# A decoder layer on one core: at the boundaries, two late squares go into the norm's sum on VectorE before TensorE sums over partitions

## The chip, the cores and the metric

The kernel runs on one core of a Trainium2 chip. A core has TensorE (PE, matrix products; PEld are its weight loads), VectorE (DVE), ScalarE (ACT), GpSimd (POOL) and SyncE (SP, which here only issues transfers). Each engine works through a queue of its own in order; they wait for each other by semaphores. The metric is the device time of one execution in microseconds.

## The reference

One decoder layer on x of 512 tokens by 1024 channels, float32. Each of three sub-layers is wrapped in two RMS norms:

```python
def rms_norm(x, g):
    y = x * lax.rsqrt(jnp.mean(x * x, axis=-1, keepdims=True) + NORM_EPS)
    return y * g

x = x + 0.5 * rms_norm(swiglu(rms_norm(x, g1), w1_in, w1_out), g1_post)
h = rms_norm(x, g2)
q, k, v, u = split(h @ w_mix_in)
mixed = concat(dilated_attention(q, k, v), s5_mixer(u)) @ w_mix_out
x = x + rms_norm(mixed, g2_post)
x = x + 0.5 * rms_norm(swiglu(rms_norm(x, g3), w2_in, w2_out), g3_post)
```

A norm needs, for every token, the sum of 1024 squares. That sum is what the change touches, at the two places where one sub-layer ends and the next begins.

## The kernel before

Activations lie transposed: channels on the 128 partitions, in 8 tiles of 128 channels (`KD` = 8), tokens along the free dimension. Every matrix product of full precision is done as three products of split operands (a high and a low half, `mm3` at L133): hence `whi`, `wlo`, `xh`, `xl` in the profile. All matmuls are issued in the written order (`mm`, L127). For other engines a planner lays out the order of each queue; `fix` (L120, `keep_in_program_order`) pins an instruction behind the one that was written before it for the same engine, and unpinned instructions go where the planner finds them ready.

`boundary` (L258) joins two sub-layers: from the first to the mix, and from the mix to the last. It works on two halves of 256 tokens (`HT`), h = 0 and 1:

- `product(h, m)` makes the last part of output tile m of the old sub-layer on TensorE (bank `yt`).
- `gather(h, m, n, b)` adds n tiles of it to `y` on VectorE (L287).
- `squares(h, m, n, eng)` squares them on ScalarE (L293) and adds the squares to `acc[h]` on the engine given (L296). Tiles 0 to 5 come in pairs: a pair's squares fill 512 columns, the even tile's in the first 256, the odd one's in the second. Tiles 6 and 7 come one by one.
- `fold` (L167) adds the second 256 columns of `acc` to the first, on GpSimd.
- `rstd` (L171) returns two steps. `sums` lets TensorE sum over the partitions (each 128x128 block of squares times a column of ones, into bank `st`), then VectorE scales (`nv`, L190) and GpSimd takes the power -1/2 (L192). `spread` lets TensorE spread the result over the partitions (bank `rp`).
- `prep(h, k)` makes tile k of the new sub-layer's input on VectorE and ScalarE: a multiply by `rp` (L302), an add to x (L304), the high half `xh` on ScalarE (L151), the low half `xl` on VectorE (L152), and its square for the next norm (ScalarE L161, added on GpSimd L163).
- `begin(h, k)` feeds that tile into the first four products of the new sub-layer (bank `first`): 12 matmuls.

In the second half the squares of tiles 0 to 5 go to `acc[1]`, which is folded after m = 5. The squares of tiles 6 and 7, 256 columns each, are not added to it: they go into the list `late`. `sums(late)` is called after `begin(0, 2)`. It lets TensorE sum three tiles into the same place: the folded `acc[1]`, and the two late ones, two blocks each, six matmuls. `spread` follows after `begin(0, 4)`, and then come `prep(1, k)` and `begin(1, k)` for k = 0 to 7.

Of the kernel before, what the change touches and what calls it, by code (L numbers as in the profile page):

```python
# [12 lines left out]
ALU = mybir.AluOpType  # L13
# [4 lines left out]
P = 128  # L18
# [10 lines left out]
HT = S // 2  # L29
# [11 lines left out]
class Layer:  # L41
# [78 lines left out]
    def fix(self, i):  # L120
        return self.tc.keep_in_program_order(i)
# [48 lines left out]
    def rstd(self, acc, y4, r, h0=0, h1=4, folded=False):  # L170

        nc = self.nc
        n = h1 - h0
        y = y4[:, h0:h1]

        def sums(more=(), fix=lambda i: i, fixp=None):

            st = self.bank("st")
            if folded and not more:
                self.fold(acc, nc.gpsimd, fixp or fix)
            t = [acc[:, 0 if folded else h0 * P:], *more]
            for i, ti in enumerate(t):
                for b in range(n):
                    self.mm(st[:, 2 * b:2 * b + 2], lhsT=ti[:, b * P:(b + 1) * P], rhs=self.ones,
                            start=i == 0 and b == 0, stop=i == len(t) - 1 and b == n - 1)
            v = self.sp.tile([P, 4], F32, name="nv", tag="nv")[:, :n]
            fix(nc.vector.tensor_scalar(out=v, in0=st[:, 0:2 * n:2], scalar1=1.0 / D, scalar2=EPS,  # L190
                                        op0=ALU.mult, op1=ALU.add))
            (fixp or fix)(nc.gpsimd.tensor_tensor(out=y, in0=v, in1=self.mhalf[:, :n], op=ALU.pow))  # L192

        def spread(fix=lambda i: i):
            rp = self.bank("rp")
            for b in range(n):
                self.mm(rp[:, b * P:(b + 1) * P], lhsT=y[:, b:b + 1].to_broadcast([P, P]),
                        rhs=self.ident, start=True, stop=True)
            if r is not None:
                fix(nc.scalar.copy(out=r[:, h0 * P:h1 * P], in_=rp[:, :n * P]))  # L200
            return rp[:, :n * P]

        return sums, spread

    def rtiles(self):
# [52 lines left out]
    def boundary(self, y, tail, ipost, half, inext, chunks):  # L258


        nc = self.nc
        w = [self.load(c, (KD, P), pool=i % 2 == 1) for i, c in enumerate(chunks)]
        tw = lambda i, m, k: self.tw[m // 2][i].rearrange("p (m k j) -> p m k j", k=NT, j=P)[:, m % 2, k]
        hs = [slice(0, HT), slice(HT, S)]
        xh, xl = self.ktiles("xh", F32R), self.ktiles("xl", F32R)
        acc2 = self.acct()
        n4, nr = self.rtiles()
        o = [self.bank("first") for _ in w]
        p4 = self.sp.tile([P, 4], F32, name="p4", tag="p4")
        bank, acc = [None], [self.acct(), self.acct()]  # L270
        post = [self.rstd(acc[h], p4, None, 2 * h, 2 * h + 2, True) for h in range(2)]
        rr = [None, None]
        pre = [self.rstd(acc2, n4, nr, 0, 2), self.rstd(acc2, n4, nr, 2, 4)]

        def product(h, m):
            if m % 2 == 0 or m == 7:
                bank[0] = self.bank("yt").rearrange("p (m t) -> p m t", m=2)
            b = bank[0][:, m % 2 if m < 6 else 0]
            for k in range(NT):
                th, tl = tail(k)  # L280
                self.mm3(b, tw(0, m, k), tw(1, m, k), th[:, hs[h]], tl[:, hs[h]], k == 0, k == NT - 1)
            return bank[0]

        def gather(h, m, n, b, fix=lambda i: i):

            ym = y.pair(slice(m, m + n))[:, :, hs[h]]
            fix(nc.vector.tensor_tensor(out=ym, in0=b[:, :n], in1=ym, op=ALU.add))  # L287

        def squares(h, m, n, eng, fix=lambda i: i):

            m2 = slice(m % 2, m % 2 + n)
            t = (acc[h] if m == 0 else self.tmp("sq")).rearrange("p (m t) -> p m t", m=2)[:, m2]
            fix(nc.scalar.activation(out=t, in_=y.pair(slice(m, m + n))[:, :, hs[h]], func=AF.Square))  # L293
            if m and eng:
                ac = acc[h].rearrange("p (m t) -> p m t", m=2)[:, m2]
                (fix if eng is V else fx)(eng.tensor_tensor(out=ac, in0=ac, in1=t, op=ALU.add))  # L296
            return t.rearrange("p m t -> p (m t)")

        def prep(h, k, fix=lambda i: i):
            t = y(k)[:, hs[h]]  # L300
            xk = self.x(k)[:, hs[h]]
            fix(nc.vector.scalar_tensor_tensor(out=t, in0=t, scalar=self.g(ipost, k, half), in1=rr[h],  # L302
                                               op0=ALU.mult, op1=ALU.mult))
            fix(nc.vector.tensor_tensor(out=xk, in0=t, in1=xk, op=ALU.add))  # L304
            self.split(xh(k)[:, hs[h]], xl(k)[:, hs[h]], xk, self.g(inext, k), fix)
            self.sq_acc(acc2[:, hs[h]], xk, k == 0, nc.gpsimd)

        def begin(h, k):
            for i in range(len(w)):
                self.mm3(o[i][:, hs[h]], w[i][0][:, k], w[i][1][:, k], xh(k)[:, hs[h]], xl(k)[:, hs[h]],  # L310
                         k == 0, k == KD - 1)

        V, G, fx = nc.vector, nc.gpsimd, self.fix
        b2 = [self.bank("yt")[:, :HT] for _ in range(2)]
        for ks in (range(NT - 1), (NT - 1,)):
            for m in range(2):
                for k in ks:
                    th, tl = tail(k)
                    self.mm3(b2[m], tw(0, m, k), tw(1, m, k), th[:, hs[0]], tl[:, hs[0]], k == 0, k == NT - 1)
        for m in range(2):  # L320
            gather(0, m, 1, b2[m].unsqueeze(1))
        squares(0, 0, 2, V)
        for m in range(2, KD):
            b = product(0, m)
            if m % 2 or m > 5:
                m, n = (m - 1, 2) if m < 6 else (m, 1)
                gather(0, m, n, b)
                squares(0, m, n, G if m == 2 else V)
        late = []
        for m in range(KD):  # L330
            b = product(1, m)
            if m % 2 or m > 5:
                m1, n = (m - 1, 2) if m < 6 else (m, 1)
                gather(1, m1, n, b)
                t = squares(1, m1, n, G if n == 2 else None)
                if n == 1:
                    late.append(t)
                if m == 5:
                    self.fold(acc[1], G, fx)
            if m == 2:  # L340
                post[0][0](fixp=fx)
            if m == 3:
                rr[0] = post[0][1]()
                for k in range(2):
                    prep(0, k)
        for k in range(KD):
            if k > 1:
                prep(0, k, fx if k > 5 else lambda i: i)
            begin(0, k)
            if k == 2:  # L350
                post[1][0](late, fix=fx)
            if k == 4:
                rr[1] = post[1][1]()
        for k in range(KD):
            prep(1, k)
            begin(1, k)
            if k == 3:
                pre[0][0](fixp=fx)
            if k == 6:
                pre[0][1]()  # L360
        self.xh, self.xl = xh, xl
        return o, n4, nr, pre[1]
# [876 lines left out]
```

## Time and profile before

| what | us |
|---|---|
| median of 3 runs (lowest, highest) | 960.45 (960.17, 960.68) |
| the profiled execution, its time | 959.66 |
| its span, from the first to the last instruction | 957.9 |
| TensorE busy | 940.9 |
| VectorE busy | 526.3 |
| ScalarE busy | 367.6 |
| GpSimd busy | 224.2 |

Times inside the trace count from the start of the span. The two boundaries lie at about 354 to 403 us and 556 to 604 us. In a row of the timeline stand the start, the duration, the engine, the line of the kernel, the operation, output and inputs, shapes and the count; in brackets is the time that the engine was idle before, and what it waited for. Matmuls overlap, so a row can start before the one ahead of it has ended; the spacing of the starts is what a matmul costs. A row of stretches gives the stretch, its length, the busy time of TensorE, its weight loads, VectorE, ScalarE and GpSimd with their counts, the granted TensorE clock (1.00 is full), the share of the DMA engines and GB/s.

### The profile page before, as it was taken

Reading aid. Unit: us, or ns where it says so; the run is one execution under the profiler, and the core shown is the slowest. Engines: PE = TensorE matmul, PEld = TensorE weight load, DVE = VectorE, ACT = ScalarE, POOL = GpSimd, SP = SyncE. Lnnn points to the kernel's source line nnn. Section 1 sums busy time; section 2 is a strip of 40 time slices with the busy share of each in tenths; the row PEclk is TensorE's granted clock in tenths of the full one; section 3 lists DMA queues with packets and bytes.
Section 4 is the critical chain, followed back from the end, with each engine's and each line's share of the span. In section 5 each row is a group of like instructions: output and inputs, shape, how many; then the busy total and the mean of one; then the engine's idle time right before and its main releaser. Section 6 shows DMA issues by size and latency. Waiting matters only on the chain.

```text
span 957.9 us, 12872 instructions
## 1 busy us (share of the span) xinstructions
PE 940.9 (98%) x5082; PEld 787.8 (82%) x5082; DVE 526.3 (55%) x934; ACT 367.6 (38%) x610; POOL 224.2 (23%) x134
## 2 busy tenths in 40 slices
PE   9999999999999999999999999999999999999995
PEld 7888888788888889988766899888888888888884
DVE  6998214463246446759896659644135524453427
ACT  7354334352233233435646645443233212232312
POOL 0234212322223233500000035421122212223300
PEclk9999999999999999999999999999999999999998
DMA  8233334353334241382313430323232232324202
GB/s 266 88 110 98 101 112 142 119 177 102 109 110 132 68 160 39 104 224 83 123 67 97 150 109 1 121 81 107 88 110 89 90 104 93 109 89 132 88 1 89
DMA packets 38173, 102.48 MB, mean 107 GB/s; under 512 B 7616, under 2 KB 10944, under 8 KB 37568
## 3 DMA queue, kind: packets, MB, share of 16 engines
q1 hardware_dynamic: 36528, 98.02, 31.6%
q10 hardware_dynamic: 1584, 3.63, 1.1%
q8 instruction: 40, 0.66, 0.3%
q14 instruction: 21, 0.17, 0.1%
HBM read 94.03 MB, written 7.60 MB: 106 GB/s over the span
## 4 chain that ended last, share of the span: by engine, by line
PE 88%; DVE 6%; ACT 2%; issue 1%; DMA 1%; POOL 0%; SPq 0%; POOLq 0%; DVEq 0%; ACTq 0%
PE gu L129 45%; PE yo L129 20%; PE yt L129 6%; PE first L129 5%; PE prj L129 3%; PE prv L129 2%; DVE wlo L104 1%; PE st L129 1%; PE ys L129 1%; PE gl L129 1%; DMA wraw<-w1i 1%; PE mo L129 1%; DVE Hs L1109 1%; DVE sx L1109 1%; PE pt L832 1%
## 5 line engine op out<-in xcount | busy, mean ns | idle before, releaser
L104 POOL TENSOR_TENSOR wlo<-wraw,whi 128x1024 fp32r<-128x1024 f32 (+2 forms) x62 | 157.3, 2537 | 496.9 <-ACT whi L102 496.8
L102 ACT CAST whi<-wraw 128x1024 fp32r<-128x1024 f32 (+5 forms) x157 | 154.6, 990 | 303.9 <-PE gu L129 118.7
L129 PE MATMUL gu<-xh,whi 128*128 128x512 f32 x656 | 257.7, 393 | 0.0
L129 PE MATMUL gu<-xh,wlo 128*128 128x512 f32 x656 | 255.7, 390 | 0.5 <-DVE wlo L104 0.5
L129 PE MATMUL gu<-xl,whi 128*128 128x512 f32 x656 | 255.3, 389 | 0.0
L104 DVE TENSOR_TENSOR wlo<-wraw,whi 128x1024 fp32r<-128x1024 f32 (+5 forms) x95 | 116.0, 1226 | 121.8 <-ACT whi L102 121.5
L129 PEld LDWEIGHTS gu<-xh,wlo 128*128 128x128 f32 x656 | 123.1, 188 | 27.0 <-DVE wlo L104 1.0
L129 PEld LDWEIGHTS gu<-xh,whi 128*128 128x128 f32 x656 | 123.2, 188 | 25.3 <-issue 0.4
L129 PEld LDWEIGHTS gu<-xl,whi 128*128 128x128 f32 x656 | 123.2, 188 | 24.9
L402 DVE TENSOR_TENSOR ut<-gu,rs 128x512 f32<-128x512 f32 x41 | 28.2, 688 | 102.8 <-PE gu L129 102.8
L149 DVE TENSOR_TENSOR al<-ut,ah 128x512 fp32r<-128x512 f32 x44 | 68.5, 1559 | 25.4 <-ACT ah L148 25.4
L400 DVE TENSOR_TENSOR gt<-gu,rs 128x512 f32<-128x512 f32 x41 | 28.2, 688 | 51.8 <-PE gu L129 51.8
L129 PE MATMUL yo<-whi,ah 128*128 128x512 f32 x144 | 56.0, 389 | 0.0
L129 PE MATMUL yo<-wlo,ah 128*128 128x512 f32 x144 | 56.0, 389 | 0.0
L129 PE MATMUL yo<-ah,whi 128*128 128x512 f32 x144 | 56.0, 389 | 0.0
L129 PE MATMUL yo<-ah,wlo 128*128 128x512 f32 x144 | 56.0, 389 | 0.0
L129 PE MATMUL yo<-whi,al 128*128 128x512 f32 x144 | 56.0, 389 | 0.0
L129 PE MATMUL yo<-al,whi 128*128 128x512 f32 x144 | 56.0, 389 | 0.0
L148 ACT CAST ah<-ut 128x512 fp32r<-128x512 f32 x44 | 27.3, 622 | 59.7 <-DVE ut L403 59.7
L129 PE MATMUL first<-xh,whi 128*128 128x256 f32 (+1 forms) x144 | 43.3, 301 | 0.4 <-ACT xh L151 0.4
L129 PE MATMUL first<-xl,whi 128*128 128x256 f32 (+1 forms) x144 | 42.6, 296 | 0.6 <-DVE xl L152 0.6
L129 PE MATMUL first<-xh,wlo 128*128 128x256 f32 (+1 forms) x144 | 42.4, 295 | 0.0
(194 smaller groups left out, 1401.9 us busy)
## 6 DMA issues: line engine op xcount, KB each, us to landing
wraw<-w2i SPq DMA_DIRECT2D x44, 512.0 KB, 3.4
wraw<-w1i SPq DMA_DIRECT2D x42, 512.0 KB, 3.5
wraw<-w2o SPq DMA_DIRECT2D x18, 512.0 KB, 3.4
wraw<-w1o SPq DMA_DIRECT2D x16, 448.0 KB, 3.4
wraw<-wmi SPq DMA_DIRECT2D x12, 512.0 KB, 3.6
x<-xT SPq DMA_DIRECT2D x8, 256.0 KB, 4.2
w1d<-w1s SPq DMA_DIRECT2D x8, 256.0 KB, 2.7
w2d<-zb SPq DMA_DIRECT2D x2, 1024.0 KB, 4.8
```

Source lines behind the costliest of these rows:

```text
L102: fix(self.nc.scalar.copy(out=hi, in_=raw))
L104: fix(eng.tensor_tensor(out=lo, in0=raw, in1=hi.bitcast(F32), op=ALU.subtract))
L129: i = self.nc.tensor.matmul(*a, **k)
L148: fix(nc.scalar.copy(out=hi, in_=src))
L149: fix(nc.vector.tensor_tensor(out=lo, in0=src, in1=hi.bitcast(F32), op=ALU.subtract))
L400: nc.vector.tensor_tensor(out=gt, in0=o[f][0], in1=r, op=ALU.mult)
L402: nc.vector.tensor_tensor(out=ut, in0=o[f][1], in1=r, op=ALU.mult)
L832: self.fix(nc.tensor.transpose(b[i][:, o:o + P], sc[:, c:c + P], self.ident))
L1109: tt = lambda o, x, y, op: self.fix(V.tensor_tensor(out=o, in0=x, in1=y, op=op))
```

## The change

The list `late` is gone. In the second half, the squares of tiles 6 and 7 are each added to the folded first 256 columns of `acc[1]` by VectorE, pinned behind what was written before them for VectorE (the gather of the same tile). `sums` always runs over one tile: two matmuls in place of six in the second half. Its first argument now only says whether it folds `acc` itself (the first half, `add=True`) or not (the second, `False`). The first half and the new sub-layer's own norms compute as before.

```diff
-        def sums(more=(), fix=lambda i: i, fixp=None):
+        def sums(add=True, fix=lambda i: i, fixp=None):
 
             st = self.bank("st")
-            if folded and not more:
+            if folded and add:
                 self.fold(acc, nc.gpsimd, fixp or fix)
-            t = [acc[:, 0 if folded else h0 * P:], *more]
-            for i, ti in enumerate(t):
-                for b in range(n):
-                    self.mm(st[:, 2 * b:2 * b + 2], lhsT=ti[:, b * P:(b + 1) * P], rhs=self.ones,
-                            start=i == 0 and b == 0, stop=i == len(t) - 1 and b == n - 1)
+            t = acc[:, 0 if folded else h0 * P:]
+            for b in range(n):
+                self.mm(st[:, 2 * b:2 * b + 2], lhsT=t[:, b * P:(b + 1) * P], rhs=self.ones,
+                        start=b == 0, stop=b == n - 1)
...
-        late = []
         for m in range(KD):
             b = product(1, m)
             if m % 2 or m > 5:
...
                 gather(1, m1, n, b)
                 t = squares(1, m1, n, G if n == 2 else None)
                 if n == 1:
-                    late.append(t)
+                    fx(V.tensor_tensor(out=acc[1][:, :HT], in0=acc[1][:, :HT], in1=t, op=ALU.add))
                 if m == 5:
                     self.fold(acc[1], G, fx)
...
             if k == 2:
-                post[1][0](late, fix=fx)
+                post[1][0](False, fix=fx)
```

## The prediction

> **What bounds the kernel now.** I read the page's share of busy time first, then busy time in stretches cut at the change, then the timelines of the engines inside one stretch.
>
> ```profile
> PE 940.9 (98%) x5082; PEld 787.8 (82%) x5082; DVE 526.3 (55%) x934; ACT 367.6 (38%) x610; POOL 224.2 (23%) x134
> 377.20:390.40 13.20, 13.20 (x114) 13.20 (x113) 11.81 (x28) 7.45 (x19) 8.49 (x10) 1.00 0.14 42
> 390.40:403.00 12.60, 12.60 (x107) 12.42 (x106) 7.78 (x19) 5.95 (x15) 5.89 (x9) 1.00 0.35 119
> 578.40:591.60 13.20, 13.20 (x114) 13.20 (x113) 11.81 (x28) 7.39 (x19) 8.45 (x10) 1.00 0.00 1
> ```
>
> Over the whole span VectorE (DVE) is half idle. In the stretch that the change edits it is not: from 377.2 to 390.4 us it works 11.81 of 13.20 us beside a TensorE that never pauses, and the same in the second boundary, 201.2 us later. So a microsecond taken from TensorE here is worth one only while VectorE still delivers its operands in time.
>
> TensorE, where the change cuts, and at the other places used below:
>
> ```profile
> 381.37 0.28 PE L129 MATMUL first<-xh,wlo 128*128 128x256 f32 x1
> 381.49 0.50 PE L129 MATMUL st<-ones,acc 128*128 128x2 f32 x4
> 381.85 1.03 PE L129 MATMUL st<-ones,sq 128*128 128x2 f32 x8
> 382.74 0.36 PE L129 MATMUL first<-xh,whi 128*128 128x256 f32 x1
> ...
> 385.70 0.60 PE L129 MATMUL rp<-ident,p 128*128 128x128 f32 x4
> ...
> 390.46 0.28 PE L129 MATMUL first<-xh,whi 128*128 128x256 f32 x1
> 390.58 0.28 PE L129 MATMUL first<-xl,whi 128*128 128x256 f32 x1
> ```
>
> Each float32 sum matmul shows as two instructions, so the six of the second half's sums are the twelve at 381.49 and 381.85. The pair at 390.46 and 390.58 is the first of `begin(1, 0)`; it reads the `xh` and `xl` that `prep(1, 0)` made.
>
> VectorE in the same stretch:
>
> ```profile
> 377.63 0.41 DVE L287 TENSOR_TENSOR y<-yt,y 128x256 f32<-128x256 f32 x1
> 377.97 0.86 DVE L302 SCALAR_TENSOR_TENSOR y<-y,gh,rp 128x256 f32<-128x256 f32 x2
> 378.75 1.02 DVE L304 TENSOR_TENSOR x<-y,x 128x256 f32<-128x256 f32 x1
> 379.69 0.41 DVE L287 TENSOR_TENSOR y<-yt,y 128x256 f32<-128x256 f32 x1
> 380.03 0.62 DVE L304 TENSOR_TENSOR x<-y,x 128x256 f32<-128x256 f32 x1
> 380.57 0.47 DVE L152 SCALAR_TENSOR_TENSOR xl<-x,sm,xh 128x256 fp32r<-128x256 f32 x1
> 380.97 0.47 DVE L302 SCALAR_TENSOR_TENSOR y<-y,gh,rp 128x256 f32<-128x256 f32 x1
> 381.47 0.56 DVE L304 TENSOR_TENSOR x<-y,x 128x256 f32<-128x256 f32 x1
> ...
> 382.63 0.48 DVE L152 SCALAR_TENSOR_TENSOR xl<-x,sm,xh 128x256 fp32r<-128x256 f32 x1 [0.20 <-ACT xh L151]
> ...
> 383.88 0.15 DVE L190 TENSOR_SCALAR nv<-st 128x2 f32<-128x2 f32 x1
> 384.55 0.48 DVE L152 SCALAR_TENSOR_TENSOR xl<-x,sm,xh 128x256 fp32r<-128x256 f32 x1 [0.51 <-ACT xh L151]
> ...
> 386.50 0.48 DVE L152 SCALAR_TENSOR_TENSOR xl<-x,sm,xh 128x256 fp32r<-128x256 f32 x1 [0.58 <-ACT xh L151]
> 386.90 0.86 DVE L302 SCALAR_TENSOR_TENSOR y<-y,gh,rp 128x256 f32<-128x256 f32 x2
> ...
> 389.30 0.57 DVE L152 SCALAR_TENSOR_TENSOR xl<-x,sm,xh 128x256 fp32r<-128x256 f32 x1
> ```
>
> The two rows at L287 with 256 columns are the gathers of m = 6 and m = 7. The rows from 377.97 to 386.50 are `prep(0, 3)` to `prep(0, 7)` (multiply, add, low half), with three short idle gaps that all wait for ScalarE's `xh`. The rows from 386.90 are `prep(1, 0)` and on. The `xl` of `prep(1, 0)` ends at 389.30 + 0.57 = 389.87; TensorE wants it at 390.58. That **0.71 us is the smallest slack** I found between the two engines behind the sums: `xl` of `prep(0, 3)` ends at 381.04 for a use near 382.94.
>
> **What is removed.** From the first sum matmul to the next product takes 382.74 - 381.49 = 1.25 us. The first four instructions, which stay, take 0.36 (381.85 - 381.49); where four stand alone the row below gives the same 0.36 to the next product (396.58 - 396.22). So 0.89 us goes from each boundary, 1.78 us from both, since the chain of waits lists the second boundary's twelve with the same 1.23 us.
>
> ```profile
> 396.22 0.50 PE L129 MATMUL st<-ones,acc 128*128 128x2 f32 x4
> 396.58 0.36 PE L129 MATMUL first<-xh,whi 128*128 128x256 f32 x1
> ...
> 381.65 1.23 PE st L129 x12
> 582.89 1.23 PE st L129 x12
> ```
>
> **What is added.** Two VectorE adds of 128x256 in each boundary. The same operation stands at L296 in the first half:
>
> ```profile
> 365.71 0.42 DVE L296 TENSOR_TENSOR acc<-acc,sq 128x256 f32<-128x256 f32 x1
> ...
> 375.42 0.41 DVE L304 TENSOR_TENSOR x<-y,x 128x256 f32<-128x256 f32 x1
> 375.76 0.96 DVE L152 SCALAR_TENSOR_TENSOR xl<-x,sm,xh 128x256 fp32r<-128x256 f32 x1
> ```
>
> One lasts 0.41 to 0.42, and the next instruction starts 0.34 behind it (375.76 - 375.42), so two in a row take 0.68 us of VectorE's queue. That is the price without any collision.
>
> **When the adds can run.** The first waits for GpSimd's fold, the second also for the square of m = 7:
>
> ```profile
> 378.19 1.30 POOL L296 TENSOR_TENSOR acc<-acc,sq 128x512 f32<-128x512 f32 x1 [1.75 <-ACT sq L293]
> 379.56 0.81 POOL L168 TENSOR_TENSOR acc<-acc 128x256 f32<-128x256 f32 x1
> 381.02 0.73 POOL L163 TENSOR_TENSOR acc<-acc,sq 128x256 f32<-128x256 f32 x1 [0.65 <-ACT sq L161]
> ...
> 380.22 0.40 ACT L293 ACTIVATE sq<-y 128x256 f32<-128x256 f32 x1
> ```
>
> The fold ends at 380.37, the square at 380.62. Put into VectorE's queue behind the add at 380.03, the two run at about 380.57 and 380.91 and end near 381.32, just before TensorE reaches the sums at 381.49. Nothing waits there. What they push back is everything queued behind: `xl` of `prep(0, 3)` from 381.04 to 381.72 (TensorE now wants it at about 382.05: fits), the rest of `prep(0, ...)`, `nv`, and then `prep(1, 0)`.
>
> A wait for a sum is also part of this. GpSimd's power follows `nv`:
>
> ```profile
> 384.12 0.71 POOL L192 TENSOR_TENSOR p<-nv,mhalf 128x2 f32<-128x2 f32 x1 [2.37 <-DVE nv L190]
> ```
>
> It ends at 384.83, for an `rp` at 385.70. TensorE will come there at 384.81. If `nv` keeps its place and slides by 0.68, TensorE waits about 0.7 us there. Stalls in sequence do not add up, though: what TensorE has lost at `rp` it no longer loses at `begin(1, 0)`. The latest gate decides, and that is `prep(1, 0)`.
>
> **The sum per boundary.** TensorE would ask for that `xl` at 390.58 - 0.89 = 389.69. It is there at 389.87 + d, plus a hop of 0.04 (below: a `wlo` that ends at 404.21 releases a matmul at 404.25), where d is how much later VectorE's chain gets there. The stall is 0.22 + d, so the gain is 0.89 - 0.22 - d = **0.67 - d**.
>
> ```profile
> 401.89 2.95 ACT L102 CAST whi<-wraw 128x1024 fp32r<-128x1024 f32 x3
> 402.97 1.23 DVE L104 TENSOR_TENSOR wlo<-wraw,whi 128x1024 fp32r<-128x1024 f32 x1 [4.25 <-ACT whi L102]
> 404.25 0.50 PE L129 MATMUL prj<-xh,wlo 128*128 128x512 f32 x1 [0.53 <-DVE wlo L104]
> ```
>
> For d, one end is 0: the three gaps (0.20 + 0.51 + 0.58 = 1.29 us) swallow the adds whole. The other is 0.68: the gaps are waits for ScalarE inside a serial chain of multiply, add, `xh`, `xl`, and the whole chain slides. I take 0.28: the chain slides by 0.68, but `rp`, today done near 386.3 (385.70 + 0.60) and so too late for the gap that ends at 386.50, comes earlier while the gap comes later, so one multiply of `prep(1, ...)` at a spacing of 0.39 (half of the pair at 386.90) can slip into it. Gain 0.67 - 0.28 = 0.39 per boundary, **0.78 for both**. At d = 0 it is 1.34, at d = 0.68 it is nothing. If the adds are queued later, behind the add at 381.47, they end near 382.7; TensorE waits 1.2 at the sums for 0.89 saved, a loss of about 0.35 per boundary, 0.7 in all.
>
> What lies behind carries a gain on: the rows above show the next stage's weights, `whi`, then `wlo`, then the matmul, released by the end of the last `begin`, so all move along with TensorE. The tiles of the late squares come free with the adds, not later than with the matmuls now, so ScalarE's squares are no worse off. DMA is 0.14 and 0.00 busy in the two stretches, so no transfer matters.
>
> The row at 378.75 shows a collision: this add lasts 1.02 us, not 0.41, and ends at 379.77, 0.28 behind the GpSimd add that ran to 379.49. If the second new add meets the GpSimd add of 0.73 us at 381.02 in the same way, d rises by up to 0.73, to between 1.01 and 1.41, and the boundary loses 0.34 to 0.74 instead of gaining. The Trainium skill, SBUF — State Buffer, section Who interferes with whom, says that a VectorE instruction with two SBUF inputs and a GpSimd instruction that reads SBUF lock each other out, the one that starts first running to its end. The row at 378.75 agrees. By that rule the add at about 380.91, which starts first, would pass and push GpSimd back.
>
> **The rivals.** *All of it is kept:* VectorE's order closes its gaps, d is below -0.2, and both boundaries keep 0.89: 1.78 us, 958.7. For it: 1.29 us of gaps. Against: the serial chain. The Trainium skill, Perfetto Trace Analysis, section Identifying the Most-Contended Engine, says to improve the engine with the highest occupancy; by that page TensorE is the one and this rival comes out.
>
> *VectorE stands still before the fold:* its queue is in order. If the first add is queued directly ahead of the add at 378.75, everything behind waits from 378.75 to 380.41, 1.66 us; d = 1.66 + 0.68 = 2.34, a loss of 1.67 per boundary, 3.3 in all. Directly behind the gather at 377.63 it waits from 377.97, 2.44 us, d = 3.12, 4.9 in all. So 963.8 to 965.4. It becomes slower by over 0.2% once the wait is above 0.95 us, so with a place ahead of 379.46. For it: the adds stand early in the program and only the gather pins the first one. Against: today's order has no wait of VectorE for GpSimd in this stretch, though nothing there depends on it.
>
> *Another order:* the planner lays out unpinned work of both boundaries again, and something else shifts by over 2 us, either way.
>
> **How the numbers follow.** The profiled execution took 959.66 us with a span of 957.9; the median of three runs is 960.45, 0.79 more. I subtract from the median: 960.45 - 0.78 = 959.67, so 959.7. A measurement of this kernel tells about 0.2%, 1.92 us, from no change, and even the whole saving is 1.78. Chances: forecast with d from 0 to collision 0.63, all kept 0.17, standing still 0.12, another order 0.08. Faster by over 0.2%: a third of all kept (scatter of the runs, 960.17 to 960.68) and half of another order, 0.10. Slower: standing still and the other half, 0.16. Within: 0.74. The range goes from the whole saving less the scatter, 958.4, to the forecast with the worst collision in both boundaries, 2 x 0.74 above the median, 961.9; a little more for the scatter, 962.0.
>
> **What would show it.** Four `st` instructions in place of twelve at the sums; two adds on VectorE at L335, between the fold and the sums; a wait of TensorE for `xl` of 0.3 to 0.9 us at the second half's first product, where it has none now, or one at `rp`. Wrong if TensorE goes through both boundaries without a wait (all kept), if a VectorE row shows a wait for GpSimd's `acc` (standing still), or if the time between the boundaries changes.

## The result, and the profile after

The changed kernel takes 962.61 us (median of 12 runs, 961.55 to 964.15), the kernel before 960.54 beside it (12 runs, 959.22 to 962.28). The ratio is 1.0021, 95% interval 1.0013 to 1.0028: about 2.07 us slower. The forecast was 959.7, and its range ended at 962.0.

The profiled execution of the changed kernel took 961.99 us with a span of 960.2. Its page, first part (busy time and instructions of each engine):

```profile
PE 941.6 (98%) x5066; PEld 787.6 (82%) x5066; DVE 528.6 (55%) x938; ACT 367.9 (38%) x610; POOL 223.4 (23%) x134
```

Sixteen matmul instructions are gone and VectorE has four more: two boundaries, eight and two each, as the diff says. The stretch that showed VectorE as the tight engine, cut at the same times (the columns are those of before):

```profile
377.20:390.40 13.20, 12.58 (x103) 12.21 (x102) 10.31 (x25) 6.30 (x16) 7.99 (x9) 1.00 0.12 42
```

VectorE got more to do and was busy 10.31 us where it was busy 11.81. An engine that has more work and does less of it in the same time is standing still; TensorE, which never paused here, now pauses too. VectorE's timeline in the first boundary, and one row of the second:

```profile
377.79 0.86 DVE L301 SCALAR_TENSOR_TENSOR y<-y,gh,rp 128x256 f32<-128x256 f32 x2
380.17 0.43 DVE L335 TENSOR_TENSOR acc<-acc,sq 128x256 f32<-128x256 f32 x1 [1.51 <-POOL acc L168]
380.51 0.42 DVE L286 TENSOR_TENSOR y<-yt,y 128x256 f32<-128x256 f32 x1
380.84 0.75 DVE L303 TENSOR_TENSOR x<-y,x 128x256 f32<-128x256 f32 x2
381.51 0.42 DVE L335 TENSOR_TENSOR acc<-acc,sq 128x256 f32<-128x256 f32 x1
...
382.24 0.59 DVE L152 SCALAR_TENSOR_TENSOR xl<-x,sm,xh 128x256 fp32r<-128x256 f32 x1
...
383.74 0.48 DVE L152 SCALAR_TENSOR_TENSOR xl<-x,sm,xh 128x256 fp32r<-128x256 f32 x1 [0.18 <-ACT xh L151]
...
385.66 0.97 DVE L152 SCALAR_TENSOR_TENSOR xl<-x,sm,xh 128x256 fp32r<-128x256 f32 x1 [0.58 <-ACT xh L151]
...
390.90 0.47 DVE L152 SCALAR_TENSOR_TENSOR xl<-x,sm,xh 128x256 fp32r<-128x256 f32 x1
...
582.69 0.43 DVE L335 TENSOR_TENSOR acc<-acc,sq 128x256 f32<-128x256 f32 x1 [1.52 <-POOL acc L168]
```

The first new add stands ahead of the last gather and of the adds to x, and waits 1.51 us for the fold; everything behind it waits too. The `xl` rows that follow are those of `prep(0, 3)`, `prep(0, 5)`, `prep(0, 6)` and `prep(1, 0)`. GpSimd beside it:

```profile
379.39 0.74 POOL L168 TENSOR_TENSOR acc<-acc 128x256 f32<-128x256 f32 x1
381.82 0.73 POOL L163 TENSOR_TENSOR acc<-acc,sq 128x256 f32<-128x256 f32 x1 [1.69 <-ACT sq L161]
384.77 0.88 POOL L191 TENSOR_TENSOR p<-nv,mhalf 128x2 f32<-128x2 f32 x1 [2.22 <-DVE nv L189]
385.62 4.68 POOL L163 TENSOR_TENSOR acc<-acc,sq 128x256 f32<-128x256 f32 x5
```

The five adds at 385.62 start 0.04 us ahead of the `xl` of `prep(0, 6)` at 385.66, which lasts 0.97 us instead of 0.48. In the kernel before it started first, at 384.55, and GpSimd's adds followed at 384.79. TensorE:

```profile
382.08 0.58 PE L129 MATMUL st<-ones,acc 128*128 128x2 f32 x4 [0.61 <-DVE acc L335]
382.52 0.36 PE L129 MATMUL first<-xh,whi 128*128 128x256 f32 x1
...
385.73 0.67 PE L129 MATMUL rp<-ident,p 128*128 128x128 f32 x4
...
391.43 0.39 PE L129 MATMUL first<-xl,whi 128*128 128x256 f32 x1 [0.59 <-DVE xl L152]
...
397.16 0.50 PE L129 MATMUL st<-ones,acc 128*128 128x2 f32 x4
...
584.60 0.58 PE L129 MATMUL st<-ones,acc 128*128 128x2 f32 x4 [0.61 <-DVE acc L335]
...
599.68 0.50 PE L129 MATMUL st<-ones,acc 128*128 128x2 f32 x4
```

To compare traces whose clocks start differently, I count from the first `rp` matmul of the boundary's first half (371.27 before, 371.09 after):

| TensorE reaches | before | after | shift |
|---|---|---|---|
| the sums | 10.22 | 10.99 | +0.77 |
| the product behind them | 11.47 | 11.43 | -0.04 |
| `rp` of the second half | 14.43 | 14.64 | +0.21 |
| the first `xl` of `begin(1, 0)` | 19.31 | 20.34 | +1.03 |
| the `st` behind `begin(1, 3)` | 24.95 | 26.07 | +1.12 |

The saving on the sums is there: TensorE comes to them 0.77 late and leaves them 0.04 early. It is lost again behind them. The first 0.25 goes ahead of `rp`, most of it at the `xl` of `prep(0, 3)`: it ends at 382.24 + 0.59 = 382.83, and the matmul that reads it starts at 382.89, 0.37 behind the one at 382.52, where the kernel before has 0.20 (382.74 to 382.94). Most of the rest goes at `begin(1, 0)`. The last number is the measure for all that follows; I call it **B**, the length of a boundary. Both boundaries give the same, 2 x 1.12 = 2.24 us, beside 2.07 in the medians and 2.3 in the spans. Outside the boundaries the spans differ by 0.1 only because larger parts cancel: the `yt` products of the second boundary take 0.55 more, the run of `ys` in the mix 0.51 less (e9 returns to both). The chain of waits (start, us, engine, tile, line), which before stays on TensorE through the whole boundary, leaves it at 371.27 for VectorE and comes back at 391.43:

```profile
371.29 0.69 DVE y L286
...
379.39 0.75 POOL acc L168
...
385.66 0.97 DVE xl L152
...
389.36 1.22 DVE x L303 x2
...
391.43 5.89 PE first L129 x47
```

**One sum explains the boundary.** The `xl` of `prep(1, 0)` ended 18.60 us after the first `rp` (389.87 - 371.27); now it ends at 20.28 (390.90 + 0.47 - 371.09). So d, as the prediction named it, is 1.68. Up to the `xl` of `prep(0, 5)` the delay is 12.65 - 11.36 = 1.29: the wait of 1.51 and the adds of 0.68, less 0.90 that VectorE no longer loses to GpSimd, mostly at the two adds to x that took 1.02 and 0.62 and now take 0.75 together. The long `xl` of `prep(0, 6)` adds 0.49, and 0.10 is saved by the last `xl` itself (0.47 for 0.57). The slack of 0.71 covers part of d. TensorE starts 0.06 behind the end of `xl`, and the matmul after that comes 0.22 later instead of 0.12, which is 0.10 more. So B changes by 1.68 - 0.71 + 0.06 + 0.10 = 1.13, or in general by **d - 0.55**, as long as this gate is what TensorE waits for. What TensorE saved does not enter that sum at all. The 0.06 and 0.10 are taken from this run; whether the rule holds elsewhere is for the experiments.

### The profile page after: what moved, and what is told of

Its sections match the earlier page's. It is cut to its first block, busy times and chain, and to the rows that moved or that the text cites. A ratio compares the mean times of both kernels' runs of the same rounds, so it can differ in the third digit from the quotient of the medians.

```text
span 960.2 us, 12844 instructions
## 1 busy us (share of the span) xinstructions
PE 941.6 (98%) x5066; PEld 787.6 (82%) x5066; DVE 528.6 (55%) x938; ACT 367.9 (38%) x610; POOL 223.4 (23%) x134
## 4 chain that ended last, share of the span: by engine, by line
PE 86%; DVE 8%; ACT 2%; issue 1%; DMA 1%; POOL 1%; SPq 0%; POOLq 0%; DVEq 0%; ACTq 0%
PE gu L129 45%; PE yo L129 20%; PE yt L129 4%; PE prj L129 3%; PE prv L129 2%; PE first L129 2%; PE mo L129 1%; DVE wlo L104 1%; PE ys L129 1%; DVE x L303 1%; PE st L129 1%; PE gl L129 1%; DVE xl L152 1%; PE sc L129 1%; PE pv L129 1%
```

## The experiments

Two questions: is it the wait at the fold, or the work put on VectorE? And is B = d - 0.55 a rule or an accident? Each ratio is to the kernel before in the same round of runs; it and its interval are taken from all runs, so it is not exactly the quotient of the medians that the text gives. The table collects what was measured; d is read in the first boundary, B in both, which agree within 0.03. In e3, e8, e9 and e10 the `xl` of `prep(1, 0)` is ready before TensorE asks for it, so the rule says nothing about their B.

| kernel | d | d - 0.55 | change of B | ratio to before (95%) |
|---|---|---|---|---|
| the change | 1.68 | 1.13 | 1.12 | 1.0021 (1.0013 to 1.0028) |
| e1, both adds later | 1.61 | 1.06 | 1.06 | 1.0027 (1.0017 to 1.0038) |
| e2, one add, no wait | 0.92 | 0.37 | 0.36 | 1.0005 (0.9996 to 1.0014) |
| e3, the wait alone | 0.85 | 0.30 | 0.35 | 1.0028 (1.0016 to 1.0041) |
| e4, no adds | -0.03 | -0.58 | -0.58 | 0.9986 (0.9977 to 0.9994) |
| e5, adds behind an `xl` | 1.24 | 0.69 | 0.68 | a single run |
| e6, adds on GpSimd | 0.56 | 0.01 | 0.00 | 1.0003 (0.9994 to 1.0011) |
| e7, sums later | 2.29 | 1.74 | 1.73 | a single run |
| e8, single pass | -0.01 | -0.56 | -0.45 | 0.9984 (0.9975 to 0.9993) |
| e9, a short wait alone | 0.16 | -0.39 | 0.24 | 1.0019 (1.0010 to 1.0028) |
| e10, e3 again | 0.84 | 0.29 | 0.34 | 1.0020 (1.0012 to 1.0029) |

**e1: both adds behind the gather of tile 7.** The changed kernel, with the first add moved one gather back. My theory then was that the wait is the loss.

```diff
                 if n == 1:
-                    fx(V.tensor_tensor(out=acc[1][:, :HT], in0=acc[1][:, :HT], in1=t, op=ALU.add))
+                    late.append(t)
+                    if m == 7:
+                        for t in late:
+                            fx(V.tensor_tensor(out=acc[1][:, :HT], in0=acc[1][:, :HT], in1=t, op=ALU.add))
```

> Both adds stay on VectorE, but both are pinned behind the gather of tile 7. In each boundary I count from the first rp matmul of the first half to the first st matmul behind begin(1, 3): 24.95 us before, 26.07 after. Theory (VectorE's wait for the fold costs, 1.51 us a boundary): the wait shrinks to about 0.35, the two adds stay, so 24.6 to 25.3 a boundary, and the time within 0.7 us of before. Rival (the two adds themselves, with their collisions with GpSimd, cost): as after, about 26, and 2 us slower than before.

962.72 us against 960.23. VectorE's timeline:

```profile
381.59 0.42 DVE L339 TENSOR_TENSOR acc<-acc,sq 128x256 f32<-128x256 f32 x1 [0.30 <-POOL acc L168]
381.93 0.48 DVE L152 SCALAR_TENSOR_TENSOR xl<-x,sm,xh 128x256 fp32r<-128x256 f32 x1
382.32 0.95 DVE L339 TENSOR_TENSOR acc<-acc,sq 128x256 f32<-128x256 f32 x1
...
386.96 0.97 DVE L152 SCALAR_TENSOR_TENSOR xl<-x,sm,xh 128x256 fp32r<-128x256 f32 x1 [0.58 <-ACT xh L151]
```

The wait is 0.30, a fifth, and B is shorter by 0.06 only: the theory fell. While VectorE doesn't wait, it runs beside GpSimd again and pays at the first add to x (1.03 us at 379.92), and the second new add lasts 0.95 because a GpSimd add of 0.81 us had started 0.13 ahead of it. The `xl` of `prep(0, 6)` is long again. A wait for GpSimd and the collisions with GpSimd stand in for each other.

**e2: one add, with no wait.** The kernel before; VectorE adds the two late tiles to each other, and the sums run over two tiles.

```diff
-                    late.append(t)
+                    if late:
+                        fx(V.tensor_tensor(out=late[0], in0=late[0], in1=t, op=ALU.add))
+                    else:
+                        late.append(t)
```

> The square of tile 7 is added to that of tile 6 on VectorE, the sums run over two tiles: one add of the same size, no wait for GpSimd, four of the eight st instructions saved (0.45 us). Theory: no wait of VectorE, 24.5 to 24.7 a boundary, about 0.7 us faster than before. Rival (the add's own price): half of the change's loss, 25.5 a boundary, 1 us slower.

960.80 against 960.23. TensorE's timeline at the two places:

```profile
381.11 0.50 PE L129 MATMUL st<-ones,acc 128*128 128x2 f32 x4
381.47 0.59 PE L129 MATMUL st<-ones,sq 128*128 128x2 f32 x4
381.92 0.36 PE L129 MATMUL first<-xh,whi 128*128 128x256 f32 x1
...
390.47 0.38 PE L129 MATMUL first<-xl,whi 128*128 128x256 f32 x1 [0.56 <-DVE xl L152]
390.69 0.28 PE L129 MATMUL first<-xh,wlo 128*128 128x256 f32 x1
```

The sums take 0.81 instead of 1.25: 0.44 saved, nothing waited for. B grows by 0.36 all the same. One add of 0.34 makes `prep(1, 0)` 0.92 late. The `xl` of `prep(0, 4)` now goes ahead of the add to x of `prep(0, 5)`, which makes that tile 0.20 later still, the `xl` of `prep(0, 6)`, at 384.70, lasts 0.97 (0.49 more), and the last `xl` gives 0.10 back. So an add on VectorE costs more here than its own length.

**e3: the wait alone.** The kernel before, and VectorE reads two columns of the folded sum into a tile that nobody uses, at the place where the change put its first add.

```diff
                     late.append(t)
+                    if m == 6:
+                        see = self.sp.tile([P, 2], F32, name="see", tag="see")
+                        fx(V.tensor_tensor(out=see, in0=acc[1][:, :2], in1=acc[1][:, :2], op=ALU.add))
```

> The kernel before with all six sum matmuls, and behind the gather of tile 6 a VectorE add of two columns of the folded sum that nothing uses: the wait without the adds and without the saving. Theory: VectorE waits 1.5 us for the fold in each boundary, 25.4 to 25.9 a boundary, 0.9 to 1.9 us slower than before. Rival (the adds cost): 24.95 a boundary, the time of before.

963.01 against 960.23. VectorE's timeline:

```profile
380.79 0.16 DVE L340 TENSOR_TENSOR see<-acc 128x2 f32<-128x2 f32 x1 [1.52 <-POOL acc L168]
...
381.21 0.75 DVE L304 TENSOR_TENSOR x<-y,x 128x256 f32<-128x256 f32 x2
...
390.60 0.57 DVE L152 SCALAR_TENSOR_TENSOR xl<-x,sm,xh 128x256 fp32r<-128x256 f32 x1
```

The same wait, 1.52, and the same two adds to x in 0.75. It delays `prep(1, 0)` by 0.85: that is the price of 1.52 of wait, half of the change's d. The 0.35 of B is not its price. The `xl` at 390.60 ends at 391.17, and TensorE reads it 0.21 later:

```profile
391.38 0.28 PE L129 MATMUL first<-xl,whi 128*128 128x256 f32 x1
```

Of the 0.35, 0.24 is there already at the first product of `begin(0, 0)`, ahead of the read that waits, and 0.11 comes at the `xl` of `prep(0, 3)`. That the rule would give 0.30 here is a coincidence. The total is another matter again: 2.78 slower, of which the boundaries explain 0.70. Neither was foreseen, and e9 and e10 return to both.

**e4: no adds.** The changed kernel without its two adds: it leaves the squares of tiles 6 and 7 of the second half out of the norm's sum. TensorE saves all, VectorE gets nothing.

```diff
-                    fx(V.tensor_tensor(out=acc[1][:, :HT], in0=acc[1][:, :HT], in1=t, op=ALU.add))
+                    pass
```

> The squares of tiles 6 and 7 of the second half are left out of the norm's sum: no adds, no matmuls for them; the saving alone. Theory (VectorE's prep(1, 0) is the next gate, 0.71 us behind): 0.67 saved a boundary, 24.28, TensorE waits about 0.2 us for xl of prep(1, 0), and 1.3 us faster than before in all. Rival (TensorE alone sets the time): 24.06 a boundary, no wait, 1.8 us faster.

958.72 against 960.23, faster. TensorE's timeline:

```profile
381.00 0.50 PE L129 MATMUL st<-ones,acc 128*128 128x2 f32 x4
381.37 0.36 PE L129 MATMUL first<-xh,whi 128*128 128x256 f32 x1
...
389.41 0.39 PE L129 MATMUL first<-xl,whi 128*128 128x256 f32 x1
389.63 0.28 PE L129 MATMUL first<-xh,wlo 128*128 128x256 f32 x1
```

The sums take 0.37, so 0.88 is saved; the `xl` of `prep(1, 0)` is where it always was and ends at 389.35 (388.78 + 0.57), 0.06 ahead of its matmul. B falls by 0.58. At d = -0.03 the rule gives 0.58 and the prediction's 0.67 - d gives 0.70. The run also gives the price of the adds in the change: 1.12 + 0.58 = 1.70 us in each boundary, for two adds that occupy 0.68.

**e5: the adds behind the `xl` of `prep(0, 3)`.** The changed kernel; `prep(0, 3)` is written ahead of the sums and both adds behind it, late enough that they find the fold done.

```diff
         for k in range(KD):
-            if k > 1:
+            if k > 1 and k != 3:
                 prep(0, k, fx if k > 5 else lambda i: i)
             begin(0, k)
             if k == 2:
+                prep(0, 3)
+                for t in late:
+                    fx(V.tensor_tensor(out=acc[1][:, :HT], in0=acc[1][:, :HT], in1=t, op=ALU.add))
                 post[1][0](False, fix=fx)
```

> Both adds on VectorE, pinned behind the xl of prep(0, 3), which is written ahead of the sums here: they come when the fold is long done. From the first rp to the st behind begin(1, 3): 24.95 us before, 26.07 after. Theory now (the boundary loses what prep(1, 0) is late by, less 0.67, whatever makes it late: waits for GpSimd, the adds, or collisions with GpSimd's adds): no wait, but 0.68 of adds, 0.2 of a changed order and 0.49 of a collision at xl of prep(0, 6), so prep(1, 0) 1.1 to 1.4 late and 25.4 to 25.7. Rival (the wait of 1.51 us for the fold is the whole loss): 24.4 to 24.95.

A single run: 962.19 against 960.31. TensorE's timeline:

```profile
383.17 0.58 PE L129 MATMUL st<-ones,acc 128*128 128x2 f32 x4 [0.76 <-DVE acc L352]
...
397.66 0.50 PE L129 MATMUL st<-ones,acc 128*128 128x2 f32 x4
```

VectorE waits for nothing of GpSimd's; TensorE waits 0.76 at the sums instead. B grows by 0.68 (397.66 - 372.03 = 25.63), as expected. This is close to the place that the prediction had assumed for the adds, and it loses too: two long low halves, 0.95 and 0.97, come on top of 0.68.

**e6: the adds on GpSimd.** The changed kernel with `G` for `V` in the line of the adds.

```diff
-                    fx(V.tensor_tensor(out=acc[1][:, :HT], in0=acc[1][:, :HT], in1=t, op=ALU.add))
+                    fx(G.tensor_tensor(out=acc[1][:, :HT], in0=acc[1][:, :HT], in1=t, op=ALU.add))
```

> The two adds are GpSimd's, behind the fold; VectorE's queue is that of before, TensorE's that of after. Theory: GpSimd works without a pause from the fold to its third add, the sums wait about 0.5 us, and VectorE's adds and xl of prep(0, 5) and (0, 4) are blocked by it for 0.5 to 0.7 in sum; 24.8 to 25.0 a boundary, time within 0.5 us of before. Rival (VectorE does nothing more, so it is not late): 24.4 to 24.6, 0.7 to 1.1 us faster than before.

961.09 against 960.31, 0.78 more where at most 0.5 was expected, but with an interval that includes no change. B is that of before, 24.95. TensorE's timeline:

```profile
382.12 0.61 PE L129 MATMUL st<-ones,acc 128*128 128x2 f32 x4 [0.54 <-POOL acc L335]
...
396.14 0.50 PE L129 MATMUL st<-ones,acc 128*128 128x2 f32 x4
```

VectorE's queue is as long as before, yet `prep(1, 0)` is 0.56 late: the longer GpSimd works beside it, the more of its instructions are long (the `xl` of `prep(0, 3)` lasts 0.97). The whole saving is given back and nothing more.

**e7: the sums later.** The changed kernel with the sums after `begin(0, 3)` and the spread after `begin(0, 5)`, so that TensorE need not wait for the adds.

```diff
-            if k == 2:
+            if k == 3:
                 post[1][0](False, fix=fx)
-            if k == 4:
+            if k == 5:
                 rr[1] = post[1][1]()
```

> The changed kernel with the sums one product later, behind begin(0, 3), and rp behind begin(0, 5). TensorE no longer waits 0.6 us at the sums. Theory (VectorE's chain decides, TensorE's stall at the sums only comes ahead of the same delay): 25.6 a boundary if the collision at xl of prep(0, 6) goes, 26.07 if it stays. Rival (the wait at the sums and at rp is the loss): 25.2 to 25.3.

A single run: 962.33 against 960.31. Neither number came out: B grows by 1.73, more than in the change. TensorE's timeline:

```profile
381.75 0.38 PE L129 MATMUL first<-xh,whi 128*128 128x256 f32 x1 [0.73 <-ACT xh L151]
...
382.44 0.39 PE L129 MATMUL first<-xl,whi 128*128 128x256 f32 x1 [0.32 <-DVE xl L152]
...
391.58 0.39 PE L129 MATMUL first<-xl,whi 128*128 128x256 f32 x1 [0.18 <-DVE xl L152]
```

The wait at the sums was no loss of its own, it was cover: with the sums out of the way TensorE waits for `prep(0, 3)` instead. And the power, coming later, moves the collisions: one add to x of `prep(0, 5)` lasts 0.95 (0.41 in the change), which is most of the 0.61 by which d exceeds the change's. The rule of d - 0.55 held even so. The total, 2.02 above before, is less than two boundaries of 1.73; a single execution doesn't tell why.

**e8: less work on TensorE, none on VectorE.** The kernel before, with ScalarE writing the two late squares in the rounded type that the low and high halves have, and a column of ones in it. Each of their matmuls is then one instruction, not two. The sum then takes these two squares rounded.

```diff
+        self.ones_r = self.cst.tile([P, 2], F32R, name="onesr")
+        nc.vector.tensor_copy(out=self.ones_r, in_=self.ones)
...
-                    self.mm(st[:, 2 * b:2 * b + 2], lhsT=ti[:, b * P:(b + 1) * P], rhs=self.ones,
+                    self.mm(st[:, 2 * b:2 * b + 2], lhsT=ti[:, b * P:(b + 1) * P], rhs=self.ones_r if i else self.ones,
...
-            t = (acc[h] if m == 0 else self.tmp("sq")).rearrange("p (m t) -> p m t", m=2)[:, m2]
+            late1 = h == 1 and n == 1
+            t = (acc[h] if m == 0 else self.tmp("sq", F32R if late1 else F32)).rearrange("p (m t) -> p m t", m=2)[:, m2]
```

> The kernel before, with the two late tiles written by ScalarE in the rounded float32 type that one matmul instruction takes in place of two; the ones for them too. No add, no wait; four of the eight st instructions go, 0.45 us. Theory: VectorE is not late, the slack of 0.71 covers it: 24.5 a boundary, 0.9 us faster than before. Rival (the instruction of this type is not shorter): 24.95, no change.

**959.15 against 960.31, ratio 0.9984 (0.9975 to 0.9993): faster than both kernels.** TensorE's timeline:

```profile
381.78 0.50 PE L131 MATMUL st<-ones,acc 128*128 128x2 f32 x4
382.14 0.58 PE L131 MATMUL st<-onesr,sq 128*128 128x2 f32 x4
382.59 0.36 PE L131 MATMUL first<-xh,whi 128*128 128x256 f32 x1
...
396.06 0.50 PE L131 MATMUL st<-ones,acc 128*128 128x2 f32 x4
```

The late sums take 0.45 (382.59 - 382.14) instead of 0.89. The 0.44 is kept whole, since it fits into the slack of `prep(1, 0)`, whose time stays what it was (d = -0.01). Half of the saving, with no work moved to the engine behind the gate, beats the whole saving with it.

**e9 and e10: a wait alone, short and long.** e9 is e3 with the unused read behind the gather of tile 7 (`m == 7`), where the wait is short; e10 is e3 a second time. They ask whether e3's total comes again.

> The kernel of the wait alone, with the same unused add of two columns pinned behind the gather of tile 7 in place of tile 6: it comes 0.8 us later in VectorE's queue, and most of what it waits for is then over. Theory (what counts is how late prep(1, 0) gets): VectorE waits about 0.3 us, less than the collision behind it gives back, so 24.95 to 25.1 a boundary, and the time within 0.3 us of before outside the scatter. Rival (any wait on GpSimd's fold costs as much, by the switch itself): 25.3 as in the wait alone.

> The wait alone once more, because its boundaries explain 0.7 us (25.30 each) and its times were 2.8 us above before, and its profile lost 1.66 us between the boundaries, where it has the same queues as before. Theory (that loss is the scatter of a stage the edit doesn't touch): 25.30 a boundary again, and the time 0.3 to 1.5 us above before. Rival (the edit costs there as well): 25.30, the same 1.7 us between the boundaries, and 2 to 3.5 us above before.

962.02 and 962.57 against 960.34. It comes again: a kernel with one 0.16 us instruction more per boundary is 1.7 us slower in e9, 2.2 in e10. VectorE's wait in e9, from its timeline:

```profile
381.34 0.16 DVE L340 TENSOR_TENSOR see<-acc 128x2 f32<-128x2 f32 x1 [0.30 <-POOL acc L168]
```

d is 0.16, and TensorE never waits for it. The 0.24 by which B grows is there at the first product after `rp`, ahead of the read, just as in e3 and e10. It belongs to the products of `yt`. From the first of these 192 matmuls to the first product of `begin(0, 0)`, TensorE takes 23.31 us in the first boundary of the nine other kernels and 23.85 in these three. In the second boundary it takes 23.35 before, 23.90 in the change, e6 and e8, 24.25 in e3 and e9 and 24.39 in e10. The one wait shown there, in the second boundary, is 0.32 before and 0.30 in e9, and in the stretches that hold these products the granted clock is 1.00 in both. The matmuls follow each other more slowly: the 42 from 372.18 to 376.94 before take 4.76 us, the same 42 in e9, from 373.13 to 378.11, take 4.98. So 0.54 + 0.90 = 1.44 us lie there in the profiled execution of e9, beside 1.7 in its medians, and as much in that of e3, with a wait of 0.30 or of 1.52 alike. What the three kernels have and the others lack is the tile `see` and its add; why the products slow down with it is not shown.

In e3 and e10 there is also one pause of TensorE in the stage of the mix that writes `ys`, 0.83 us in e10 and 0.76 in e3, whose chain of waits has it after 228 matmuls:

```profile
527.08 6.46 PE ys L129 x228
533.53 0.76 issue
```

"issue" means that the engine waited for nothing that the profile shows. The kernel before has the same pause, 0.11 long, e9 one of 0.02, e6 of 0.44 and e1 of 0.76; the change has none. In e1 and e6 it comes after 236 matmuls of `ys`, and these kernels have eight matmul instructions fewer ahead of it: in all six it stands ahead of the program's matmul instruction number 2893. (e5 has one of 0.30, 128 matmul instructions later.) So it belongs to a place in TensorE's instruction stream and not to the wait. What happens there, and why it lasts 0 to 0.83 us, no run here tells. So neither the totals nor B of e3, e9 and e10 are used for the price of the wait; d is, where the engines' rows show what waits for what.

## Why the prediction was wrong

- **What is removed: right.** 0.89 was forecast for a boundary; the sums of e4 take 0.37 where they took 1.25, 0.88.
- **The gate: right.** `prep(1, 0)` with 0.71 us of slack decides, not `rp` (0.21 late in the change, with no wait shown) and not the sums. Stalls in sequence do not add up: the 0.77 at the sums is no part of the 1.12. Right too is the form of the sum, 0.67 - d. The terms of it are off by the hop (0.06 and 0.10 instead of 0.04), so 0.55 - d; e4 kept 0.58 at d = -0.03.
- **"Put into VectorE's queue behind the add at 380.03 ... Nothing waits there": the step that failed.** I placed the adds where they would find the fold done. The first one is pinned behind the gather of its own tile, and it went directly ahead of the add at 378.75, the place that the rival *VectorE stands still* had named. It waits 1.51 (that rival: 1.66); the row at 380.17 is the sign that the prediction had named for being wrong, a VectorE row that waits for GpSimd's `acc`. From that place, d, taken as 0.28 with 0.68 as the bound without collisions and 1.41 as the worst with one, became 1.68.
- **Would the right place have saved it? Probably not.** The exact place was not run. e5 put the adds a little behind it, where VectorE does not wait for the fold, and d was 1.24, not 0.28. The second failed step is the treatment of collisions as one possible mishap. In this stretch GpSimd was busy 8.49 of 13.20 us beside VectorE's 11.81, and 0.34 us of queue moves the pairs that meet: e2's single add made `prep(1, 0)` 0.92 late. The multiply that was to slip into a gap was not what mattered; the `xl` of `prep(0, 6)`, 0.97 for 0.48 in the change, e1, e2 and e5, was.
- **The rival that came nearest was mispriced as well.** *VectorE stands still* gave 1.67 per boundary, 963.8 to 965.4. It added the wait to the adds in full. But a VectorE that waits for GpSimd doesn't collide with it meanwhile: e3's wait of 1.52 makes `prep(1, 0)` 0.85 late, and e1, without most of the wait, loses the same as the change. The time came out between the forecast and this rival.
- **All of it is kept: wrong.** Without the adds (e4), 0.58 of 0.88 is kept; with them, less than nothing. A saving on TensorE counts here as far as the next engine's slack reaches, 0.71 us. The Trainium skill, Perfetto Trace Analysis, section Identifying the Most-Contended Engine, says to optimize the engine with the highest occupancy first and to judge TensorE by its weight loads, here 82% beside VectorE's 55%. It names TensorE, but not how much of a saving there is kept.
- **Who passes whom.** The Trainium skill, SBUF — State Buffer, section Who interferes with whom, has whichever of the two starts first go through. The traces agree: the change's second add started at 381.51, ahead of GpSimd's at 381.82, and took 0.42; e1's started 0.13 behind GpSimd's and took 0.95.

## What to carry to other kernels

Work taken from the busiest engine was worth no more here than the slack of the engine that feeds it next, so find that slack first, and don't pay with work on that same engine: 0.44 saved for nothing (e8) was worth more than 0.89 saved for two adds. Before pricing a wait, find where the planner will put the waiting instruction, by what it is pinned behind, and price it by how late the last gate becomes, not by its length. Where two engines lock each other out, a wait for the other and collisions with it are substitutes, and any shift of the queue deals the collisions anew. A probe is a change too: before using its total, compare a stage that runs ahead of it.

## What the runs showed of the hardware that was not expected

- The same 192 matmuls of `yt`, up to the first product behind them, take 23.31 to 24.39 us, depending on the kernel and the boundary. The granted clock is 1.00 both before and in e9, and waits shown do not account for more than 0.14 of it. It is not explained.
- A pause of TensorE of up to 0.83 us that waits for nothing shown stands ahead of matmul instruction number 2893 in six kernels, also where fewer matmuls ahead of it put that number at another product. It is not explained.
- After a wait, the second matmul comes 0.22 us behind the first (389.41 to 389.63 in e4, 390.47 to 390.69 in e2) where the usual spacing is 0.12, so a short wait costs 0.10 more than it shows.
- A sum matmul of two columns in float32 costs its two instructions 0.11 us each (0.89 for eight), and in the rounded type one of 0.11 (0.45 for four).
